# Down projection of a gated MLP by one level of Strassen's scheme, in three sweeps over PSUM

## The chip, the cores and the metric

One NeuronCore of a Trainium2 chip runs the whole program. The metric is device time in microseconds (us) of one execution; a lower number is better. The engines are named as the profile names them: PE (TensorE), DVE (VectorE), ACT (ScalarE), POOL (GpSimd) and SP (SyncE, which issues most transfers).

## The reference

One layer of a post-norm encoder, 512 tokens of 1024 channels: a token mixer (pooling, latent attention and a spatial gate), then a gated MLP. All numbers are float32. What the change touches is the end:

```python
def _conv_ffn(h, w_up, conv_w, conv_b, w_down):
    z = h @ w_up                                  # (512, 1024) @ (1024, 5632)
    ...                                           # causal depthwise convolution over three tokens
    val, gate = jnp.split(zc, 2, axis=-1)
    return (jax.nn.silu(gate) * val) @ w_down     # (512, 2816) @ (2816, 1024)

# in reference():
y = _conv_ffn(h, w_up[l], conv_w[l], conv_b[l], w_down[l])
x = _layer_norm(ALPHA * x + gt_f[:, None, :] * y) * ln_f_g[l] + ln_f_b[l]
```

gt_f is one row of 1024 numbers, the sublayer's gate, made from the condition c.

## The kernel before

Every product keeps float32 accuracy with a faster matmul type: each operand is split into a high part (a cast on ACT) and a low part (a subtraction on DVE), and mm3 issues three matmuls, high x low, low x high and high x high, onto one bank of PSUM. A matmul has 128 rows of contraction, 128 columns of the left operand and 512 of the right.

A scheduler fixes the order of the instructions on each engine when the program is built, from its own estimate of times; on the chip each engine then takes its list in that order and waits where an operand is missing.

The up projection runs over 22 chunks i of 128 hidden columns (NP = 22), value and gate half, 24 matmuls each. The epilogue of a chunk is: scale and bias on ACT out of PSUM, two DVE instructions for the other taps of the convolution (tiles zc), silu on ACT, the product of value and gate on POOL (L1203), then the split into f{i}h and f{i}l, which lie transposed: hidden columns on partitions, 512 tokens in the free dimension.

The down projection is the call of project_out at the end. It holds all eight banks of PSUM (tiles pyd: four token tiles by two halves of the 1024 output columns). For each chunk k it loads 128 rows of w_down (512 KB, by SP, into a buffer raw of which there are three), multiplies them by gt_f on POOL in two halves of 512 columns (scaled_chunk, L936), splits them (L940 on ACT, L941 on DVE), and issues 24 matmuls. The last four chunks are kept resident, so that the token tiles come to their end one after the other, and finish(t) of a tile (residual, LayerNorm, gain and bias, store) runs beside the matmuls of the next; only the last one has nothing beside it.

The row of gt_f is made beside the up projection (ada_piece, ada_rows). Tiles of the tags pt (8 buffers of 512 columns), h (16), act (48), and whi and wlo (two of 1024 columns each) are handed round.

## Time and profile before

| what | us |
|---|---|
| three runs | 1021.66, 1024.28, 1024.99; median 1024.28 |
| profiled execution, first to last instruction (span) | 1018.8 |
| median less span | 5.5 |
| PE busy in the span | 973.7 (96%) |
| DVE, ACT, POOL busy | 611.4, 384.2, 325.7 |
| first matmul of the down projection starts | 888.71 |
| its last matmul ends | 1010.34 |

The page lists no time of the profiled execution beside its span. Times in the text are us from the start of the span. A row of the time line has start, duration, engine, line, operation, output and inputs, and in brackets how long the engine sat idle before it and what ended that. A row of a group has the count, then busy time and mean ns. Line numbers are those of the kernel before.

### The profile page before, as it was taken

To read this page: it belongs to the slowest core of one execution; us is meant where nothing else is said; L and a number is where in the kernel's file an instruction comes from. 1 tells how busy PE (TensorE), PEld (TensorE's weight loads), DVE (VectorE), ACT (ScalarE), POOL (GpSimd) and SP (SyncE) were. 2 spreads that over 40 slices of the span, in tenths; PEclk is the share of its full clock that TensorE was granted. 3 is DMA by queue.
4 is the path that set the end of the run, shared out by engine and by line. 5 is a ranking of instruction groups with operands and counts; after the bars stand their busy time and mean duration, and the time that the engine had idled before them with its cause. 6 is when DMAs were issued, how large, how long until landed. Compare 5 with 4: busy or idle time off the path is not lost.

```text
span 1018.8 us, 12189 instructions
## 1 busy us (share of the span) xinstructions
PE 973.7 (96%) x4496; PEld 797.4 (78%) x4496; DVE 611.4 (60%) x931; ACT 384.2 (38%) x650; POOL 325.7 (32%) x340
## 2 busy tenths in 40 slices
PE   4789999999999999999999999899999999999996
PEld 3677778777888877788888877898888888888885
DVE  7957555548446377763343578676666665633267
ACT  3365454542224322332322233664443443412221
POOL 5564111121242054120001575512111121466664
PEclk9999999999999999999999999999999999999998
DMA  9612111118324226652223255113433343342322
GB/s 336 259 40 91 47 50 50 57 42 279 114 83 124 89 80 211 202 184 87 79 83 104 83 169 203 42 62 113 136 124 112 116 145 85 99 137 94 103 83 83
DMA packets 45276, 119.20 MB, mean 117 GB/s; under 512 B 5280, under 2 KB 8736, under 8 KB 45216
## 3 DMA queue, kind: packets, MB, share of 16 engines
q1 hardware_dynamic: 45072, 118.30, 35.8%
q8 instruction: 35, 0.57, 0.2%
q14 instruction: 25, 0.20, 0.1%
q10 hardware_dynamic: 144, 0.12, 0.0%
HBM read 116.30 MB, written 2.10 MB: 116 GB/s over the span
## 4 chain that ended last, share of the span: by engine, by line
PE 73%; DVE 9%; POOL 6%; DMA 6%; issue 4%; ACT 2%; SPq 0%; DVEq 0%; POOLq 0%; ACTq 0%
PE pzu L97 7%; PE pzu L99 7%; PE pzu L98 7%; PE pg L98 4%; PE pyd L97 4%; PE pg L99 4%; PE pg L97 4%; PE pyd L99 4%; PE pyd L98 4%; PE pu L97 3%; PE pu L99 3%; PE pu L98 3%; PE py L98 2%; PE py L99 2%; PE py L97 2%
## 5 line engine op out<-in xcount | busy, mean ns | idle before, releaser
L1203 POOL TENSOR_TENSOR zc<-zc 128x512 f32<-128x512 f32 x22 | 32.8, 1489 | 178.9 <-ACT zc L1202 178.9
L936 POOL TENSOR_TENSOR d<-d,gtfb 128x512 f32<-128x512 f32 x44 | 72.8, 1677 | 41.9 <-DMA d<-in_wdn 39.5
L298 POOL TENSOR_TENSOR mg<-mg,th 128x512 f32<-128x512 f32 x16 | 25.0, 1562 | 139.7 <-DVE th L295 120.2
L1188 DVE SCALAR_TENSOR_TENSOR zc<-pzu,cols,zc 128x511 f32<-128x511 f32 x44 | 32.8, 747 | 52.4 <-ACT zc L1185 52.4
L1185 ACT ACTIVATE zc<-pzu,cols 128x512 f32<-128x512 f32 x44 | 34.2, 779 | 72.2 <-PE pzu L99 72.2
L941 DVE TENSOR_TENSOR dl<-d,dh 128x1024 fp32r<-128x1024 f32 x18 | 29.9, 1660 | 52.3 <-ACT dh L940 52.3
L679 DVE SCALAR_TENSOR_TENSOR ada<-adar,cact,ada 128x512 f32<-128x512 f32 x56 | 52.9, 970 | 13.2 <-DMA adar<-in_ada 13.2
L90 ACT CAST wbh<-wb 128x1024 fp32r<-128x1024 f32 x24 | 25.2, 1050 | 65.7 <-PE py L99 57.2
L91 DVE TENSOR_TENSOR wgl<-wg,wgh 128x1024 fp32r<-128x1024 f32 x22 | 27.3, 1243 | 35.3 <-ACT wgh L90 34.1
L91 DVE TENSOR_TENSOR wupl<-wup,wuph 128x1024 fp32r<-128x1024 f32 x38 | 46.6, 1227 | 0.0
L91 DVE TENSOR_TENSOR wbl<-wb,wbh 128x1024 fp32r<-128x1024 f32 x24 | 35.1, 1461 | 16.3 <-ACT wbh L90 16.1
L91 DVE TENSOR_TENSOR wsgl<-wsg,wsgh 128x1024 fp32r<-128x1024 f32 x16 | 19.6, 1223 | 39.4 <-ACT wsgh L90 39.4
L940 ACT CAST dh<-d 128x1024 fp32r<-128x1024 f32 x18 | 18.9, 1051 | 60.7 <-PE pyd L99 60.6
L90 ACT CAST wuph<-wup 128x1024 fp32r<-128x1024 f32 x38 | 39.5, 1039 | 0.0
L278 ACT ACTIVATE th<-pg 128x512 f32<-128x512 f32 x22 | 13.1, 597 | 61.8 <-PE pg L99 61.8
L113 POOL TENSOR_SCALAR pw<-mv 128x1 f32<-128x1 f32 x20 | 8.2, 408 | 82.5 <-DVE mv L122 69.6
L90 ACT CAST wsgh<-wsg 128x1024 fp32r<-128x1024 f32 x16 | 16.8, 1049 | 47.0 <-PE pu L99 44.9
L1192 DVE SCALAR_TENSOR_TENSOR zc<-pzu,cols,zc 128x510 f32<-128x510 f32 x44 | 32.7, 747 | 1.3
L936 POOL TENSOR_TENSOR o<-o,gttb 128x512 f32<-128x512 f32 x16 | 27.0, 1712 | 17.5 <-DVE th L295 9.8
L734 POOL TENSOR_TENSOR asum<-apad 128x527 f32<-128x527 f32 x8 | 9.1, 1141 | 59.2 <-ACT apad L729 25.9
L600 POOL TENSOR_SCALAR pe<-pe,mx 128x128 f32<-128x128 f32 (+3 forms) x32 | 17.4, 553 | 33.4 <-DVE mx L599 33.2
L201 DVE SCALAR_TENSOR_TENSOR acc<-ada,cact,acc 128x256 f32<-128x256 f32 x48 | 27.8, 638 | 0.0
(1369 smaller groups left out, 3230.0 us busy)
## 6 DMA issues: line engine op xcount, KB each, us to landing
wup<-in_wup SPq DMA_DIRECT2D x44, 512.0 KB, 3.5
adar<-in_ada SPq DMA_DIRECT2D x64, 256.0 KB, 3.8
wb<-in_wb SPq DMA_DIRECT2D x24, 512.0 KB, 3.5
wg<-in_wg SPq DMA_DIRECT2D x22, 512.0 KB, 3.5
d<-in_wdn SPq DMA_DIRECT2D x22, 512.0 KB, 3.5
ada<-in_ada SPq DMA_DIRECT2D x32, 256.0 KB, 4.8
wsg<-in_wsg SPq DMA_DIRECT2D x16, 512.0 KB, 3.5
wa<-in_wa SPq DMA_DIRECT2D x8, 512.0 KB, 3.5
```

What stands on the lines that cost most here:

```text
L90: nc.scalar.copy(out=hi[:, :n], in_=raw[:, :n])
L91: nc.vector.tensor_tensor(out=lo[:, :n], in0=raw[:, :n], in1=f(hi[:, :n]), op=ALU.subtract)
L97: nc.tensor.matmul(o, wh, xl, start=start, stop=False)
L98: nc.tensor.matmul(o, wl, xh, start=False, stop=False)
L99: nc.tensor.matmul(o, wh, xh, start=False, stop=stop)
L679: nc.vector.scalar_tensor_tensor(out=acc[n], in0=src, scalar=cact[:, k : k + 1], in1=acc[n], op0=ALU.mult, op1=ALU.add,)
L936: nc.gpsimd.tensor_tensor(out=raw[:, c], in0=raw[:, c], in1=gt[n], op=ALU.mult)
L941: nc.vector.tensor_tensor(out=lo, in0=raw, in1=f(hi), op=ALU.subtract)
L1185: nc.scalar.activation(t, pz, AF.Identity, bias=cols[:, cc + 3 : cc + 4], scale=cols[:, cc + 2 : cc + 3])
L1188: nc.vector.scalar_tensor_tensor(out=t[:, 1:512], in0=pz[:, 0:511], scalar=cols[:, cc + 1 : cc + 2], in1=t[:, 1:512], op0=ALU.mult, op1=AL ...
L1192: nc.vector.scalar_tensor_tensor(out=t[:, 2:512], in0=pz[:, 0:510], scalar=cols[:, cc : cc + 1], in1=t[:, 2:512], op0=ALU.mult, op1=ALU.add,)
L1203: nc.gpsimd.tensor_tensor(out=val, in0=val, in1=gate, op=ALU.mult)
```

## The change

The down projection takes chunks in pairs q (NQ = 11): chunk 2q and chunk 2q + 1. With the tokens halved (rows 0 to 255 and 256 to 511) and the output columns halved, each pair is a 2 x 2 block product: A11, A21 are the halves of f{2q}, A12, A22 those of f{2q+1}; B11, B12 are the column halves of chunk 2q of w_down, B21, B22 those of chunk 2q + 1. Seven block products take the place of eight, and a block product is six matmuls (two token tiles by three):

| sweep | bank | left | right |
|---|---|---|---|
| 1 | P1 | A11 | B11 |
| 1 | P5 | A21 - A22 | B11 + B12 |
| 1 | P6 | A21 - A22 - A11 | B11 + B12 + B22 |
| 1 | P4 | A22 | B11 + B12 + B21 + B22 |
| 2 | onto P1 | A12 | B21 |
| 2 | onto P5 | A12 - A22 - (A11 - A21) | B22 |
| 3 | onto P6 | A11 - A21 | B12 + B22 |

Each row is summed over the 11 pairs. Between sweep 1 and the next, P1 is copied to SBUF (m1, ACT) and three sums with it are kept: v = P5 - P1, u = P6 + P1, w = P4 + P1 (DVE, out of PSUM). The four output blocks are sums of P1, P5, P6 with u, v, w. gt_f multiplies u, v, w (fold, on POOL) and the banks at the end (finish, on DVE) and no longer the weights.

Sums on the left are made by pair_up (POOL, three of 256 columns a pair) beside the up projection, and in second_operands. Sums of the weights are made on POOL in sweep 1, three of 512 columns a pair. B12 + B22 is made by third_sum: SP loads B12 into a raw buffer and POOL issues a second transfer that adds B22 to it while it lands. The weights are loaded once in sweep 1, the odd chunks again in sweep 2, and the right halves again for sweep 3. finish gets two more DVE instructions a tile, and for the tiles 0 to 2 the form with scale and bias on ACT and gain and bias on POOL and DVE.

The diff, cut to its core:

```diff
+    def pair_up(q):
+        fe, fo = f_t[2 * q], f_t[2 * q + 1]
+        s12 = pad_t("s12")
+        nc.gpsimd.tensor_tensor(out=s12[:, :256], in0=fe[:, 256:], in1=fo[:, 256:], op=ALU.subtract)
+        nc.gpsimd.tensor_tensor(out=s12[:, 256:512], in0=s12[:, :256], in1=fe[:, :256], op=ALU.subtract)
+        nc.gpsimd.tensor_tensor(out=fe[:, 256:], in0=fe[:, :256], in1=fe[:, 256:], op=ALU.subtract)
...
+    def third_sum(q):
+        x = wp.tile([P, D], F32, name="wdn3", tag="raw", bufs=3)
+        nc.sync.dma_start(out=x[:, :512], in_=wdn(2 * q, 1))
+        nc.gpsimd.dma_start(out=x[:, :512], in_=wdn(2 * q + 1, 1), accum_op=ALU.add)
+        t3[q] = halves_split([x[:, :512]], act_t, f"t3{q}")
+    for q in range(NQ):
+        fe, fo = f_t[2 * q], f_t[2 * q + 1]
+        r0 = load(A["wdn"][2 * q * P : (2 * q + 1) * P, :], D, "wdn")
+        r1 = [pt_t(f"wdn{n}") for n in range(2)]
+        for n in range(2):
+            nc.sync.dma_start(out=r1[n], in_=wdn(2 * q + 1, n))
+        nc.gpsimd.tensor_tensor(out=r0[:, 512:], in0=r0[:, :512], in1=r0[:, 512:], op=ALU.add)
+        nc.gpsimd.tensor_tensor(out=r1[1], in0=r1[1], in1=r0[:, 512:], op=ALU.add)
+        nc.gpsimd.tensor_tensor(out=r1[0], in0=r1[0], in1=r1[1], op=ALU.add)
...
+        product(P1, (ah[:, :256], al[:, :256]), (h0[:, :512], l0[:, :512]), first, final)
+        product(P5, (sh[:, :256], sl[:, :256]), (h0[:, 512:], l0[:, 512:]), first, final)
+        product(P6, (sh[:, 256:], sl[:, 256:]), (h1[1], l1[1]), first, final)
+        product(P4, (ah[:, 256:], al[:, 256:]), (h1[0], l1[0]), first, final)
+        if q:
+            third_sum(q - 1)
...
+    for q in range(NQ - RES):
+        ops = second_operands(q)
+        for i in range(2):
+            second(q, i, ops)
+        if q == 0:
+            fold("u", 1, 0, ALU.subtract)
...
     def finish(t, banks):
...
         for n in range(2):
+            nc.vector.tensor_tensor(out=dst[n], in0=banks[n], in1=gt_f[n], op=ALU.mult)
+            if t < 2 and n == 0:
+                nc.vector.scalar_tensor_tensor(
+                    out=dst[n], in0=x1[t][n], scalar=ALPHA, in1=dst[n], op0=ALU.mult, op1=ALU.add
+                )
+            else:
+                nc.vector.tensor_tensor(
+                    out=dst[n], in0=x1[t][n], in1=dst[n],
+                    op=ALU.subtract if t >= 2 and n == 1 else ALU.add,
+                )
             nc.vector.bn_stats(out=st[:, n, :], in_=dst[n])
...
-    project_out(
-        lambda k: A["wdn"][k * P : (k + 1) * P, :], NP, 4, a_hi, a_lo, gt_f, h_t, finish, "d"
-    )
+    for q in range(NQ - RES, NQ):
+        stay[q] = second_operands(q)
+    for i in range(2):
+        for q in range(NQ - RES, NQ):
+            second(q, i, stay[q])
+        finish(i, (P1[i], P5[i]))
+    for i in range(2):
+        c = slice(i * P, (i + 1) * P)
+        l = slice(256 + i * P, 256 + (i + 1) * P)
+        for q in range(NQ):
+            (th,), (tl,) = t3[q]
+            mm3(P6[i], s3[q][:, c], s3[q][:, l], th, tl, False, q == NQ - 1, True)
+        finish(2 + i, (P6[i], P6[i]))
```

The order of the built program holds 528 pyd matmuls before and 462 now. Three places of it matter to the prediction.

First, POOL at the seam of up and down projection. Before, zc is the product of value and gate of a chunk (the third row is that of the last chunk), and d a piece of weights times the gate:

```order
L936 TENSOR_TENSOR d<-d,gtfb_7157 128x512
L936 TENSOR_TENSOR d<-d,gtfb_7159 128x512
L1203 TENSOR_TENSOR zc<-zc 128x512
L936 TENSOR_TENSOR d<-d,gtfb_7157 128x512
L936 TENSOR_TENSOR d<-d,gtfb_7159 128x512
```

Now f_7502 and f_7575 are those products of the last two chunks, s_7577 the tile s12 of the last pair, wdn the weight sums of pairs 0 to 2:

```order
L1223 TENSOR_TENSOR f_7502<-zc 128x512
L1250 DMA wdn_7693<-in_wdn 128x512
L1261 TENSOR_TENSOR wdn_7596<-wdn_7596,wdn 128x512
L1223 TENSOR_TENSOR f_7575<-zc 128x512
L1262 TENSOR_TENSOR wdn_7595<-wdn_7595,wdn_7596 128x512
L1261 TENSOR_TENSOR wdn_7645<-wdn_7645,wdn 128x512
L1177 TENSOR_TENSOR s_7577<-f_7502,f_7575 128x256
L1260 TENSOR_TENSOR wdn<-wdn 128x512
L1262 TENSOR_TENSOR wdn_7644<-wdn_7644,wdn_7645 128x512
L1178 TENSOR_TENSOR s_7577<-s_7577,f_7502 128x256
```

The sums of pairs 0 to 2 stand between the last chunk's product and the last pair's s12. ACT at the same place, now:

```order
L1281 CAST a1h<-f_6054 128x256
L1182 CAST s10h<-s_7577 128x512
L1281 CAST a1h<-f_6133 128x256
L1281 CAST a0h<-f_5920 128x256
L1281 CAST a0h<-f_5987 128x256
```

The left operand of the first pair, a0h, stands behind the cast of the last pair's s12; PE's first row of the stage is `L97 MATMUL pyd<-wdnl,a0h 128x512`.

Second, POOL in the middle of sweep 1, now (two pairs; the L1250 rows are the adding transfers of third_sum):

```order
L1260 TENSOR_TENSOR wdn<-wdn 128x512
L1261 TENSOR_TENSOR wdn_7935<-wdn_7935,wdn 128x512
L1250 DMA wdn_7983<-in_wdn 128x512
L1262 TENSOR_TENSOR wdn_7934<-wdn_7934,wdn_7935 128x512
L1260 TENSOR_TENSOR wdn<-wdn 128x512
L1261 TENSOR_TENSOR wdn_7993<-wdn_7993,wdn 128x512
L1250 DMA wdn_8041<-in_wdn 128x512
L1262 TENSOR_TENSOR wdn_7992<-wdn_7992,wdn_7993 128x512
```

Where POOL had two products a chunk (the rows L936 above, four a pair), it has three sums and a transfer a pair, the transfer ahead of the last sum.

Third, the end of DVE's list. Before, these are the rows behind the one that reads the last matmul's bank (out_8360 is the second half of token tile 3), with that row first:

```order
L1219 SCALAR_TENSOR_TENSOR out_8360<-x_31_5451,pyd 128x512
L1222 BN_STATS st<-out_8360 128x6
L1224 BN_AGGR mv<-st 128x2
L1228 SCALAR_TENSOR_TENSOR out_8360<-out_8360,mv,lnfg_7565 128x512
L1228 SCALAR_TENSOR_TENSOR out_8359<-out_8359,mv,lnfg_7563 128x512
L1240 SCALAR_TENSOR_TENSOR out_8360<-out_8360,rs,lnfb_7569 128x512
L1240 SCALAR_TENSOR_TENSOR out_8359<-out_8359,rs,lnfb_7567 128x256
```

Now the last matmul's bank is read by the second row here (out_8632, token tile 1); out_8688 and out_8689 are token tile 2, and 28 rows follow the second, of which these are the first:

```order
L1365 TENSOR_TENSOR out_8631<-pyd,gtfb_7173 128x512
L1365 TENSOR_TENSOR out_8632<-pyd,gtfb_7175 128x512
L1365 TENSOR_TENSOR out_8688<-pyd,gtfb_7173 128x512
L1367 SCALAR_TENSOR_TENSOR out_8631<-x_10_5340,out_8631 128x512
L1365 TENSOR_TENSOR out_8689<-pyd,gtfb_7175 128x512
L1371 TENSOR_TENSOR out_8632<-x_11_5341,out_8632 128x512
L1371 TENSOR_TENSOR out_8688<-x_20_5404,out_8688 128x512
L1375 BN_STATS st<-out_8631 128x6
```

On PE the last matmul onto P6 (token tiles 2 and 3) stands 60 matmuls ahead of the last of all, which goes onto P5 of token tile 1.

145 lines of the change are left out of this document (124 added, 21 removed).

## Prediction

> **What bounds the kernel now.** I read the page first (busy shares, slices, chain), then the time line of the down projection by engine, then the groups by shape.
>
> ```profile
> span 1018.8 us, 12189 instructions
> PE 973.7 (96%) x4496; PEld 797.4 (78%) x4496; DVE 611.4 (60%) x931; ACT 384.2 (38%) x650; POOL 325.7 (32%) x340
> PEclk9999999999999999999999999999999999999998
> PE 73%; DVE 9%; POOL 6%; DMA 6%; issue 4%; ACT 2%; SPq 0%; DVEq 0%; POOLq 0%; ACTq 0%
> ```
>
> PE is busy for 96% of the span, the granted clock is full until the last slice, and PE carries 73% of the chain that ended last. In the stage that is changed PE has no gap. Two rows of the time line, the first matmul of the 24 of one chunk and of the next, and the busy times of ten microseconds of this stage (span stretch, then PE, PEld, DVE, ACT, POOL busy with their counts, clock, DMA share, GB/s):
>
> ```profile
> 966.23 0.40 PE L97 MATMUL pyd<-dl,f14h 128*128 128x512 f32 x1
> 971.72 0.39 PE L97 MATMUL pyd<-dl,f15h 128*128 128x512 f32 x1
> ```
> ```profile
> 920.00:930.00 10.00, 10.00 (x45) 8.24 (x44) 2.42 (x2) 2.10 (x2) 6.55 (x6) 1.00 0.34 107
> ```
>
> 5.49 us for 24 matmuls is 0.2288 us each. Beside it POOL is busy 6.55 of 10 us and DVE only 2.42, so matmuls are the price of this stage and POOL is the engine with the least room.
>
> **Matmuls: a gain of 15.1 us.** 528 become 462; 66 x 0.2288 = 15.1 us, all on the path as long as PE stays the bound. No other term below is a gain, except 0.8 us of idle PE that before has in the stage (888.71 to 1010.34 is 121.6 us, 528 x 0.2288 is 120.8).
>
> **The start: a loss of 13.3 us.** Where the stage begins today:
>
> ```profile
> 888.71 0.50 PE L97 MATMUL pyd<-dl,f0h 128*128 128x512 f32 x1 [0.45 <-DVE dl L941]
> ```
> ```profile
> 890.73 0.64 ACT L1202 ACTIVATE zc<-zc 128x512 f32<-128x512 f32 x1 [0.72 <-DVE zc L1192]
> 892.30 2.54 POOL L936 TENSOR_TENSOR d<-d,gtfb 128x512 f32<-128x512 f32 x2 [4.74 <-DMA d<-in_wdn]
> 894.80 1.29 POOL L1203 TENSOR_TENSOR zc<-zc 128x512 f32<-128x512 f32 x1
> ```
>
> The first down matmul runs at 888.71, right behind the up projection, since f0 was split long ago. The gating product of the last chunk, f21 (POOL, L1203), has its input at 891.37 (890.73 + 0.64) but starts at 894.80, because POOL takes its instructions in their order and two weight pieces stand ahead of it. Nothing waits for f21 then. In the changed order something does: PE's first down matmul reads a0h, ACT casts a0h after s10h, s10h needs s12 of the last pair, and that needs f21. So the first matmul waits for the end of the up projection's epilogue and for POOL's rows up to L1178. Prices alone, by shape:
>
> ```profile
> L936 POOL TENSOR_TENSOR d<-d,gtfb x44: 1283/1302/2334, 874.6 to 986.6; 128x512 f32<-128x512 f32 x44
> L941 DVE TENSOR_TENSOR dl<-d,dh x18: 1218/1578/2325, 886.5 to 978.5; 128x1024 fp32r<-128x1024 f32 x18
> L947 ACT CAST d18h<-d x2: 622/622/622, 975.5 to 976.7; 128x512 fp32r<-128x512 f32 x2
> L948 DVE TENSOR_TENSOR d20l<-d,d20h x2: 1565/1568/1571, 984.0 to 985.7; 128x512 fp32r<-128x512 f32 x2
> L83 SPq DMA_DIRECT2D d<-in_wdn x22: 327/328/328, 870.0 to 980.4; - x22
> DMA to landing us min/median/max: 3.2/3.5/4.6
> ```
> ```profile
> L1238 POOL TENSOR_TENSOR out<-out,lnfb 128x256 f32<-128x256 f32 x1 | 0.7, 747 | 0.6 <-ACT out L1237 0.6
> L125 POOL TENSOR_SCALAR rs<-mv,rs 128x1 f32<-128x1 f32 x16 | 6.0, 376 | 1.2
> ```
> ```profile
> L948 DVE TENSOR_TENSOR o4l<-o,o4h 128x512 fp32r<-128x512 f32 x2 | 1.3, 680 | 0.0
> L104 DVE TENSOR_TENSOR PTl<-ptp,PTh 128x256 fp32r<-128x256 f32 x8 | 3.2, 404 | 0.0
> L1228 DVE SCALAR_TENSOR_TENSOR out<-out,mv,lnfg 128x512 f32<-128x512 f32 x8 | 5.7, 749 | 0.1
> L1222 DVE BATCH_NORM_STATS2 st<-out 128x6 f32<-128x512 f32 x8 | 5.5, 691 | 0.2
> ```
> ```profile
> L508 ACT CAST qst<-qro 128x256 fp32r<-128x256 f32 x8 | 2.9, 405 | 3.8 <-POOL qro L501 3.8
> L1237 ACT ACTIVATE out<-out,rs 128x512 f32<-128x512 f32 x3 | 2.2, 725 | 17.9 <-POOL rs L116 17.9
> ```
>
> (The rows of tile d give least, median and most in ns; the others the mean.) POOL: 1.30 for 512 columns, 0.75 for 256. DVE: 1.22 for 1024, 0.69 for 512, 0.40 for 256, all undisturbed. ACT: 0.62 and 0.41. From 891.4 POOL has five of 512 columns and two of 256, 8.0 us, to 899.4; ACT's s10h, a1h and a0h take 1.44 to 900.8. DVE disturbs POOL twice in that time (next part), and four handovers between engines come on top: I take 902. The bounds are 900.8 and 904. 902 - 888.7 = 13.3.
>
> **What DVE and POOL cost each other.** The price of an operation is not its price alone here. The median of d20l is 1.57 us where o4l, the same shape, took 0.68. The place:
>
> ```profile
> 981.82 6.56 POOL L936 TENSOR_TENSOR d<-d,gtfb 128x512 f32<-128x512 f32 x4 [0.26 <-DMA d<-in_wdn]
> ```
> ```profile
> 983.96 3.28 DVE L948 TENSOR_TENSOR d20l<-d,d20h 128x512 fp32r<-128x512 f32 x2
> ```
>
> Four POOL operations took 6.56 us back to back (1.64 each) with one DVE operation beside each. Alone the pair would be 1.30 + 0.69 = 1.99 one after the other; so two busy engines pass through in 1.64 / 1.99 = 0.82 of their summed time, nearly as if they took turns. [...]
>
> **Sweep 1: a loss of 7.4 us.** From 891.4 on it still needs on POOL: f21, nine sums of r0, ten and eleven of the two halves of r1 (31 x 1.30) and three of 256 columns (2.3): 42.6. DVE: ten low parts of 1024 (12.2), 34 of 512 (22 of r1, 11 of the third sums, s10l: 23.5) and 22 of 256 (8.8): 44.5. Together 87.1, x 0.82 = 71.4: to 962.8. PE, begun at 902, needs 264 x 0.2288 = 60.4: to 962.4. So both are full, and anything that leaves one of them without work adds. That is the third sum: its plain load waits for a raw buffer, POOL's accumulating transfer waits for the load and holds POOL's queue (the r1 sum of the next pair stands behind it), then ACT, then DVE, ahead of the next l0. One round for two pairs: chunk load 3.5 and 0.33 to issue, two POOL sums of 1.64 (disturbed), the accumulating transfer, cast 0.62, subtraction 1.57. The accumulating transfer has no row. Nearest, 256 KB and the slowest single load (KB, us to landing):
>
> ```profile
> adar<-in_ada SPq DMA_DIRECT2D x64, 256.0 KB, 3.8
> wqr<-in_wqr SPq DMA_DIRECT2D x1, 512.0 KB, 6.9
> ```
>
> I take 3.8, the same size, and 6.9 as the far end; 0 would be the near end. With 3.8 the round is 13.1 us, 6.55 a pair, against 5.49 on PE: 1.06 x 7 pairs, once the first four are through, is 7.4. End of sweep 1 at 969.8, 7.4 later than PE alone; bounds 0 and, at 6.9 (3.1 more a round, 1.55 more a pair), 18.3. The Trainium skill (DMA: Bandwidth & Descriptors, Latency and other measured facts) puts the first byte of a transfer that GpSimd generates at about 1 us against 0.6; by it the round would be 0.4 longer and the sum 1.4 us higher; no row here shows it.
>
> **Sweeps 2 and 3: a loss of 6 us.** 198 matmuls, 45.3 us, are mixed by the order (P6's fill the waits of P1 and P5). Operands: POOL 22 sums of 256 and six gate products, 16.5 + 7.8 = 24.3; DVE 33 of 256 (13.2), eight of 1024 (9.8), six of 512 (4.1), six folds of 0.75 and six subtractions from PSUM of 0.69 (8.6): 35.7. 60.0 x 0.82 = 49.2, begun some 3 us before sweep 1 ends: to 1016. About 24 matmuls (5.5 us) come behind the last operand: last matmul at 1021, some 6 later than PE alone (1015.1). Bounds 0 and 17 (factor 1.0). ACT has a cast of 1.05 and five of 0.41 a pair, 3.1 us in the 4.1 that PE takes, and a chunk of 512 KB lands in 3.5: nothing for either.
>
> **The end: a loss of 19.5 us.** Now:
>
> ```profile
> 1009.94 0.40 PE L99 MATMUL pyd<-d21h,f21h 128*128 128x512 f32 x1
> 1010.38 0.69 DVE L1219 SCALAR_TENSOR_TENSOR out<-x,pyd 128x512 f32<-128x512 f32 x1 [0.53 <-PE pyd L99]
> 1011.10 0.69 DVE L1222 BATCH_NORM_STATS2 st<-out 128x6 f32<-128x512 f32 x1
> 1011.83 0.21 DVE L1224 BATCH_NORM_AGGREGATE mv<-st 128x2 f32<-128x12 f32 x1
> 1012.07 1.42 DVE L1228 SCALAR_TENSOR_TENSOR out<-out,mv,lnfg 128x512 f32<-128x512 f32 x2
> 1012.13 0.75 POOL L113 TENSOR_SCALAR pw<-mv 128x1 f32<-128x1 f32 x1 [1.60 <-DVE mv L1224]
> 1012.96 0.94 POOL L116 TENSOR_TENSOR rs<-pw,neghalf 128x1 f32<-128x1 f32 x1
> 1013.93 1.61 DVE L1240 SCALAR_TENSOR_TENSOR out<-out,rs,lnfb 128x512 f32<-128x512 f32 x2 [0.44 <-POOL rs L116]
> 1014.51 0.75 POOL L1238 TENSOR_TENSOR out<-out,lnfb 128x256 f32<-128x256 f32 x1 [0.62 <-ACT out L1237]
> ```
>
> The last matmul ends at 1010.34, seven DVE rows follow, and the span closes 3.3 us after the last of them, 8.5 in all. In the changed order the tiles of tokens 256 to 511 are ready 60 matmuls early, but their rows stand on DVE behind the gate product of token tile 1 that reads the last matmul's bank. So 31 DVE instructions follow it or run at its end: 22 of about 0.72 with the gap (15.8), four of 0.75 (3.0), the three aggregations and a half row (1.1), the first one 0.7: 20.6 us; five or six of them meet POOL's gain and bias products, and POOL's own chain (two pairs of row statistics at 0.75 + 0.94 + 0.38, three full products, then the last tile's 0.75 + 1.30 + 0.94 + 0.75, with ACT at 0.73 between) ends near 25. With 3.3 behind it: 28, against 8.5. Bounds 23 and 31.
>
> **Edits that cost nothing.** The gate on the weights goes (44 POOL products of 1.30 to 1.64), but POOL's new sums are in the ledgers above. pair_up on POOL (three of 256 columns a pair) lies beside 96 up matmuls, some 22 us, in which POOL has two products else; without that cover it would be 2.3 us a pair.
>
> **Sum.** -15.1 - 0.8 + 13.3 + 7.4 + 6 + 19.5 = +30.3: span 1018.8 -> 1049. The page gives no time of its execution beside the span; the median of the runs is 1024.28, 5.5 above it (launch and end, carried over): 1024.3 + 30.3 = 1054.6, said as 1055.
>
> **Rivals.** (a) The sweeps run at PE's pace, since DVE and POOL overlap better than in the one place I could read: last matmul at 902 + 105.7 = 1007.7, 1041 in all. For it: the ledgers come out level with PE at 0.82. Against: the round of the third sum. (b) Full turns, factor 1.0: sweep 1's operands to 891.4 + 87.1 = 978.5, those of sweep 2 to 1038.5, the last matmul 5 later, time about 1077. [...] (c) The accumulating transfer at 6.9: 10.9 us more: 1066. (d) Faster: PE stays the bound throughout; the waits in the ledgers, at the start and at the end are hidden and 15.1 comes through: 1009. It decides once all waits together stay under 15.1 us; the order gives 32.8 at the two ends alone, so both readings would have to be wrong. (e) The matmuls aren't fewer: excluded by the order's count of 462.
>
> **Chances.** Mine, 1046 to 1062: 0.47. (a) 0.22; (b) 0.09; (c) 0.12; (d) 0.06; partly (d), no change within 0.3% (3 us, about what a measurement here tells apart): 0.04. Slower 0.90, same 0.04, faster 0.06. The range 1036 to 1075 takes in (a), mine and (c) and leaves out (b), (d) and no change.
>
> **What would show it.** The first pyd matmul near 902, behind ACT's a0h, with POOL busy before it; in sweep 1 a pair every 6.6 us, PE waiting for DVE's low parts, and DVE's 512 columns at 1.0 to 1.6; sweep 1 over at 970; last matmul at 1021; then 28 us with PE idle and DVE full. I am wrong if PE has no gap at 889, or the span closes within 12 us of the last matmul.

## The result, and the profile after

The changed kernel takes 1075.1 us (median of four runs, 1073.8 to 1076.5) against 1023.0 for the kernel before on the same chip: a ratio of 1.051, 95% interval 1.049 to 1.053. Slower was forecast, at 1055 with a range of 1036 to 1075; the time is 20 us above the forecast and just outside the range. Three lines of the page after:

```profile
span 1073.4 us, 12434 instructions
...
PE 977.5 (91%) x4430; PEld 792.4 (74%) x4430; DVE 684.2 (64%) x1024; ACT 416.2 (39%) x731; POOL 373.1 (35%) x407
...
PEclk9899999999999999999999989999999997999895
```

The span is 1073.4, 54.6 longer than before. PE went from 96% busy to 91%. Its granted clock (a digit for each 26.8 us, in tenths) shows 7 and 8 in two slices of the down projection, 886 to 912 and 993 to 1020, where before had 9, and 5 in the last one, where PE is idle. Next, the three stretches that the prediction prices, as windows of the profile after: first sweep (first product to last), second and third sweep (to the last matmul), and close. The columns are stretch and length, then busy time and count of PE, PEld, DVE, ACT and POOL, granted clock, DMA share and GB/s:

```profile
902.20:990.10 87.90, 72.05 (x264) 53.27 (x264) 62.57 (x65) 36.81 (x69) 46.61 (x40) 0.91 0.60 159
990.10:1046.20 56.10, 50.15 (x199) 38.88 (x198) 46.56 (x66) 19.39 (x40) 28.32 (x26) 0.94 0.34 104
1046.20:1073.40 27.20, 0.00 (x0) 0.00 (x0) 22.26 (x30) 4.96 (x7) 14.67 (x17) 0.58 0.21 77
```

The loss of each is what it took beyond its matmuls at 0.2288 us each; the end is compared with the 8.5 us of before.

| loss against PE alone, us | predicted | measured | from |
|---|---|---|---|
| start | 13.3 | 13.5 | first product at 902.2 |
| first sweep | 7.4 | 27.5 | 87.9 less 264 x 0.2288 |
| sweeps two and three | 6 | 10.8 | 56.1 less 198 x 0.2288 |
| end | 19.5 | 18.7 | 27.2 less 8.5 |
| fewer matmuls, idle time before | -15.9 | -15.9 | |
| sum on the span | +30.3 | +54.6 | |

In the first sweep neither DVE (62.6 of 87.9 us) nor POOL (46.6) is full, and still PE waits. From the list of waits (who waits for whom: us in all, times, longest), and the idle time ahead of PE's rows on the time line:

```profile
PE pyd L97 <- ACT a0h L1281: 13.5, 1, 13.5
...
POOL wdn L1260 <- DMA wdn<-in_wdn: 21.9, 6, 8.6
...
POOL wdn L1250 <- DMA wdn<-in_wdn: 11.3, 3, 5.3
...
ACT t33h L1235 <- DMA wdn<-in_wdn: 9.3, 1, 9.3
```
```profile
902.24 1.22 PE L97 MATMUL pyd<-wdnl,a0h 128*128 128x512 f32 x2 [13.52 <-ACT a0h L1281]
...
916.96 0.50 PE L97 MATMUL pyd<-wdnl,a1h 128*128 128x512 f32 x1 [1.23 <-DVE wdnl L1266]
...
925.92 0.50 PE L97 MATMUL pyd<-wdl,s3h 128*128 128x512 f32 x1 [3.15 <-DVE wdl L1236]
...
944.00 0.50 PE L97 MATMUL pyd<-wdnl,s5h 128*128 128x512 f32 x1 [2.82 <-DVE wdnl L1266]
```

PE waits for DVE's low parts (wdnl, wdl), as foretold; but behind that stand POOL, which waits for transfers, and ACT, which waits for the third sum's. The wait of 3.15 us at 925.92, followed back, in order of time:

```profile
914.73 0.69 DVE L1236 TENSOR_TENSOR t31l<-wdn,t31h 128x512 fp32r<-128x512 f32 x1 [6.13 <-ACT t31h L1235]
915.45 0.33 SPq L83 DMA_DIRECT2D wdn<-in_wdn  x1
919.32 1.28 POOL L1260 TENSOR_TENSOR wdn<-wdn 128x512 f32<-128x512 f32 x1 [8.60 <-DMA wdn<-in_wdn]
922.66 4.91 DVE L1236 TENSOR_TENSOR wdl<-wdn,wdh 128x512 fp32r<-128x512 f32 x2 [4.62 <-ACT wdh L1235]
```

The low part of a third sum, late because ACT waited for its transfer, gives a raw buffer free at 915.42. SP issues the next row load at once (the trace names t31l as what released it), and POOL has stood 8.60 us for that row. Then POOL's sums come in a burst, and beside them two low parts take 4.91 us, where two alone take 1.28. PE goes on behind the first of them. The wait of 2.82 us at 944.00 stands behind one slow transfer: the adding transfer issued at 932.37 landed 7.4 us later (least, median and most of the eleven: 3.7, 4.3 and 7.4), and t33h, for which ACT stood 9.3 us, is its cast.

The last matmul and the last DVE rows:

```profile
1045.76 0.40 PE L99 MATMUL pyd<-wr10h,c10h 128*128 128x512 f32 x1
```
```profile
1067.92 1.61 DVE L1402 SCALAR_TENSOR_TENSOR out<-out,rs,lnfb 128x512 f32<-128x512 f32 x2
```

### The profile page after: what moved, and what is told of

Same layout as the page of the kernel before. It is cut to its first block, busy times and chain, and to the rows that moved or that the text cites. A ratio compares the mean times of both kernels' runs of the same rounds, so it can differ in the third digit from the quotient of the medians.

```text
span 1073.4 us, 12434 instructions
## 1 busy us (share of the span) xinstructions
PE 977.5 (91%) x4430; PEld 792.4 (74%) x4430; DVE 684.2 (64%) x1024; ACT 416.2 (39%) x731; POOL 373.1 (35%) x407
## 5 line engine op out<-in xcount | busy, mean ns | idle before, releaser
L1223 POOL TENSOR_TENSOR f<-zc 128x512 f32<-128x512 f32 x22 | 33.4, 1519 | 158.5 <-ACT zc L1221 158.5
L679 DVE SCALAR_TENSOR_TENSOR ada<-adar,cact,ada 128x512 f32<-128x512 f32 x56 | 55.7, 1021 | 13.2 <-DMA adar<-in_ada 13.1
L90 ACT CAST wbh<-wb 128x1024 fp32r<-128x1024 f32 x24 | 25.2, 1050 | 65.7 <-PE py L99 57.2
L91 DVE TENSOR_TENSOR wgl<-wg,wgh 128x1024 fp32r<-128x1024 f32 x22 | 27.3, 1243 | 35.3 <-ACT wgh L90 34.2
L91 DVE TENSOR_TENSOR wbl<-wb,wbh 128x1024 fp32r<-128x1024 f32 x24 | 35.2, 1465 | 16.3 <-ACT wbh L90 16.1
L278 ACT ACTIVATE th<-pg 128x512 f32<-128x512 f32 x22 | 13.1, 597 | 61.8 <-PE pg L99 61.8
L936 POOL TENSOR_TENSOR o<-o,gttb 128x512 f32<-128x512 f32 x16 | 26.9, 1702 | 18.2 <-DMA o<-in_wo 14.0
L1236 DVE TENSOR_TENSOR wdl<-wdn,wdh 128x512 fp32r<-128x512 f32 x20 | 24.7, 1255 | 8.2 <-ACT wdh L1235 7.6
L90 ACT CAST wgh<-wg 128x1024 fp32r<-128x1024 f32 x22 | 23.2, 1052 | 11.6 <-PE pu L99 5.7
L201 DVE SCALAR_TENSOR_TENSOR acc<-ada,cact,acc 128x256 f32<-128x256 f32 x48 | 26.8, 616 | 0.0
L1260 POOL TENSOR_TENSOR wdn<-wdn 128x512 f32<-128x512 f32 x11 | 15.9, 1447 | 29.0 <-DMA wdn<-in_wdn 21.9
```

The costliest lines, as they stand in the source:

```text
L90: nc.scalar.copy(out=hi[:, :n], in_=raw[:, :n])
L91: nc.vector.tensor_tensor(out=lo[:, :n], in0=raw[:, :n], in1=f(hi[:, :n]), op=ALU.subtract)
L201: nc.vector.scalar_tensor_tensor(out=acc[i], in0=src, scalar=cact[:, k : k + 1], in1=acc[i], op0=ALU.mult, op1=ALU.add,)
L679: nc.vector.scalar_tensor_tensor(out=acc[n], in0=src, scalar=cact[:, k : k + 1], in1=acc[n], op0=ALU.mult, op1=ALU.add,)
L936: nc.gpsimd.tensor_tensor(out=raw[:, c], in0=raw[:, c], in1=gt[n], op=ALU.mult)
L1223: nc.gpsimd.tensor_tensor(out=fi, in0=val, in1=gate, op=ALU.mult)
```

## The experiments

Each layer experiment was timed beside the kernel before. "First" is the length of the first sweep, "2+3" from its end to the last matmul, "close" from there to the span's end, all from the one profiled execution of that run. For e3 and e6 that execution took 1068.5 and 1070.3 us, 3.6 and 4.7 above the median. e8 and e12 edit nothing in the first sweep, and it takes 84.9 and 83.9 us there, after a start 4.0 and 2.9 later; so a difference of 3 to 4 us in one stage is not read as an effect of an edit.

| run | time | ratio to before (95%) | first product | first | 2+3 | close |
|---|---|---|---|---|---|---|
| changed kernel | 1075.1 | 1.051 (1.049-1.053) | 902.2 | 87.9 | 56.1 | 27.2 |
| e1 | 1069.4 | 1.045 (1.042-1.048) | 905.9 | 81.3 | 52.6 | 27.7 |
| e2 | 1064.2 | 1.040 (1.038-1.043) | 902.5 | 76.7 | 54.4 | 27.7 |
| e3 | 1064.9 | 1.042 (1.039-1.045) | 902.4 | 76.3 | 60.3 | 27.8 |
| e4 | 1076.8 | 1.053 (1.050-1.056) | 908.8 | 84.7 | 57.3 | 26.9 |
| e5 | 1048.6 | 1.025 (1.024-1.027) | 900.0 | 62.8 | 56.6 | 28.0 |
| e6 | 1065.6 | 1.043 (1.041-1.046) | 905.0 | 78.8 | 56.9 | 27.8 |
| e7 | 1069.6 | 1.046 (1.044-1.048) | 892.5 | 92.2 | 57.4 | 27.3 |
| e8 | 1070.1 | 1.047 (1.045-1.048) | 906.2 | 84.9 | 57.5 | 19.7 |
| e9 | 1023.3 | 1.001 (0.999-1.002) | | | | |
| e10 | 1039.1 | 1.016 (1.014-1.018) | 893.1 | 70.5 | 54.3 | 20.2 |
| e11 | 1038.8 | 1.016 (1.014-1.019) | 890.6 | 76.4 | 46.5 | 23.5 |
| e12 | 1071.5 | 1.048 (1.046-1.050) | 905.1 | 83.9 | 52.2 | 28.8 |
| e13 | 1034.4 | 1.012 (1.010-1.014) | 890.0 | 70.8 | 46.5 | 23.5 |
| e14 | 1032.3 | 1.009 (1.006-1.013) | 890.7 | 71.2 | 46.4 | 21.8 |

### What paces the first sweep: e1 to e6

**e1**, another place for the third sum's tile:

```diff
-        x = wp.tile([P, D], F32, name="wdn3", tag="raw", bufs=3)
+        x = pad_t("wdn3")
```

> The tile into which third_sum loads and accumulates takes a buffer of the pad kind (five, idle in the first sweep) in the place of one of the three raw buffers that the row loads use; nothing else is edited. Theory A (the first sweep of the products, 88 us in the changed kernel against 60.4 us of matmuls, is paced by the ring of three raw buffers: a row load waits until a third sum has been loaded, accumulated, copied and subtracted): the row loads come one pair earlier and the sweep takes 70 to 78 us, so 1057 to 1065 us against 1075. Rival B (the pace is VectorE and GpSimd sharing a port, the sum on which my forecast rested): the same work on both, so 1073 to 1077 us. Rival C (the accumulating transfer itself, 3.3 to 4.2 us from issue to landing, on which ScalarE waits in order): nothing of it is removed, so 1070 to 1077 us.

6.6 us of the sweep and 5.7 of the time: less gain than A gives, more than B, and just more than C. (The sweep starts 3.7 later, so its end comes only 2.9 earlier.) The time line shows what came up behind the ring. DVE and POOL of e1, around PE's longest wait in that sweep:

```profile
931.99 3.53 DVE L1236 TENSOR_TENSOR wdl<-wdn,wdh 128x512 fp32r<-128x512 f32 x1 [5.77 <-ACT wdh L1235]
935.44 3.47 DVE L1236 TENSOR_TENSOR t34l<-wdn,t34h 128x512 fp32r<-128x512 f32 x1
```
```profile
931.00 1.53 POOL L1260 TENSOR_TENSOR wdn<-wdn 128x512 f32<-128x512 f32 x1
932.22 1.52 POOL L1262 TENSOR_TENSOR wdn<-wdn,wdn 128x512 f32<-128x512 f32 x1
933.45 1.51 POOL L1261 TENSOR_TENSOR wdn<-wdn,wdn 128x512 f32<-128x512 f32 x1
```

A low part that takes 0.68 alone stands with 3.53 us while POOL runs sums at its own pace of 1.23 from start to start.

**e2**, no accumulating transfer:

```diff
-        nc.gpsimd.dma_start(out=x[:, :512], in_=wdn(2 * q + 1, 1), accum_op=ALU.add)
```

> Leaves out the accumulating transfer of third_sum (eleven of 256 KB, issued by GpSimd), so the third operand is B12 alone; loads, casts and products stay. A: a raw buffer is held some 5 us shorter for each pair, and the ring turns faster, 8 to 15 us of the sweep: 1060 to 1067 us. B: GpSimd loses 11 issues of 0.88 us that move no data through the shared port: 1072 to 1076 us. C: the sweep goes to nearly the matmuls' own pace, 62 to 68 us: 1050 to 1056 us.

A's number. C, the transfer's own time as the one cause (1050 to 1056), is out: without any adding transfer the sweep still takes 76.7. How the gain divides into the buffer held, POOL's queue and the wait for the landing, e2 does not show.

**e3**, no sums of weights on POOL:

```diff
-        nc.gpsimd.tensor_tensor(out=r0[:, 512:], in0=r0[:, :512], in1=r0[:, 512:], op=ALU.add)
-        nc.gpsimd.tensor_tensor(out=r1[1], in0=r1[1], in1=r0[:, 512:], op=ALU.add)
-        nc.gpsimd.tensor_tensor(out=r1[0], in0=r1[0], in1=r1[1], op=ALU.add)
```

> Leaves out the three sums of down weights that GpSimd makes for each pair (33 instructions of 128x512, lines 1260 to 1262), so the products run on the raw rows; all transfers stay. A: the transfers and the raw buffers set the pace, so at most 8 us of the sweep goes: 1067 to 1075 us. B: GpSimd's 33 x 1.2 us no longer share the port, VectorE runs free, and the sweep goes to the matmuls' pace, 62 to 66 us: 1049 to 1054 us. C: as A, 1068 to 1075 us.

Between A and B. **e5**, e1's and e3's edits together:

> e1 and e3 together: third_sum's tile in the pad kind, and the three GpSimd sums of weights of each pair left out (the products run on the raw rows). In e1 the first sweep took 81.3 us, in e3 76.3, against 87.9 in the changed kernel. If two limits lie one behind the other (A, the raw ring with its in-order queues; B, GpSimd keeping VectorE from the port), each hides the gain of removing the other, and both together bring the sweep to 61 to 66 us: 1048 to 1055 us. If a third thing sets the pace (the clock that falls after gaps, SP's queue, ScalarE), the sweep stays above 70 us and the time above 1058 us.

Two limits that hide each other: 6.6 us of the sweep for the one alone, 11.6 for the other, 25.1 for both (5.7, 10.2 and 26.5 us of the time), and the sweep is 2.4 us from PE alone. Those 2.4 are the clock: PE is busy for all of the 62.8 us, at a granted 0.96. The first sweep as one window in e1, e3 and e5:

```profile
905.90:987.20 81.30, 69.37 (x265) 53.95 (x266) 71.10 (x72) 39.21 (x71) 52.31 (x40) 0.89 0.60 167
```
```profile
902.40:978.70 76.30, 66.01 (x264) 51.65 (x264) 40.02 (x63) 31.87 (x60) 11.87 (x15) 0.95 0.67 180
```
```profile
900.00:962.80 62.80, 62.80 (x265) 51.44 (x266) 43.63 (x70) 38.20 (x71) 15.78 (x17) 0.96 0.79 234
```

In e1 DVE is busy for 71.1 of 81.3 us (72 instructions), in e5 for 43.6 of 62.8 (70): the 27.5 us between them are, nearly all, what DVE's instructions take longer beside POOL's sums. In e3 DVE is at 40.0 of 76.3 and POOL at 11.9: neither is full, and as e5 differs from e3 only in the third sum's tile, it is the raw ring with its transfers that costs 13.5 us there. One thing e3 and e5 leave together: without the sums, POOL's step between transfer and cast is gone as well as its load on the port. No run parts these two.

**e4** works the third operand out of sums in SBUF:

```diff
-        x = wp.tile([P, D], F32, name="wdn3", tag="raw", bufs=3)
-        nc.sync.dma_start(out=x[:, :512], in_=wdn(2 * q, 1))
-        nc.gpsimd.dma_start(out=x[:, :512], in_=wdn(2 * q + 1, 1), accum_op=ALU.add)
-        t3[q] = halves_split([x[:, :512]], act_t, f"t3{q}")
+        r0, s = raws.pop(q)
+        x = r0[:, :512]
+        nc.gpsimd.tensor_tensor(out=x, in0=s, in1=x, op=ALU.subtract)
+        t3[q] = halves_split([x], act_t, f"t3{q}")
```

> Works the third operand out from what is in SBUF: B12+B22 is the second sum (B11+B12+B22) less B11, one GpSimd subtraction of 128x512 in place of two transfers and a raw buffer for each pair; same output. A: the raw ring serves row loads alone and the sweep takes 66 to 74 us: 1053 to 1062 us. B: GpSimd gets 11 x 1.2 us more on the shared port: 1078 to 1088 us. C: as A or better, 1050 to 1058 us.

A's gain does not come, and B's range, from 1078, begins just above the 1076.8. The sweep is 3.2 us shorter after a start 6.6 later. The edit takes no raw buffer for the third sum, but it does not free the loads: the row and the sum that POOL subtracts must now stay until it has done so. SP's loads of r1 stood 24.6 us in six waits (the longest 10.9) for that subtraction, and the row loads stand behind them on SP. Eleven POOL instructions more go to the port besides. One limit was loaded in the place of another.

**e6**, the three sums on DVE (`nc.vector` for `nc.gpsimd` in e3's three lines):

> The three sums of weights of each pair go from GpSimd to VectorE; same output. B (GpSimd's instructions keep VectorE out, and a 0.68 us instruction becomes 1.8 to 3.5 us): VectorE's pair is 4.0 + 3 x 0.68 = 6.0 us undisturbed against the 7.4 of the changed kernel, the sweep 72 to 78 us (the ring is still there, e3 had 76.3): 1060 to 1067 us. The ledger of my forecast (the summed time of both engines times 0.82 is what counts, and it falls only by 3 x (1.3 - 0.68) a pair): 1064 to 1070 us. A alone: 1073 to 1077 us.

A alone is refuted (9.5 us gained with the same transfers); B's range and the ledger's both hold 1065.6, so e6 does not tell these two apart.

### What the port costs: m1, m2, m3

> Not the layer: a short program of chains, read from its trace alone. Sixteen additions of 128x512 (f32, both operands in SBUF) on VectorE alone, sixteen on GpSimd alone, then 32 on VectorE beside 16 on GpSimd; the same with GpSimd in pauses, with one VectorE operand in PSUM, with one tensor operand only, with ScalarE copies in VectorE's place; four accumulating transfers of 256 KB one after the other; eight runs of 60 matmuls with 0 to 8 VectorE additions between them. Strict turns (B): beside each other one addition of each in 0.6 + 1.25 = 1.85 us, so 16 GpSimd additions take 30 us. The factor 0.82 of my forecast: 1.52 us, 24 us. Starving (GpSimd keeps the port from one addition to the next): 20 us with two or three VectorE additions in them. An operand in PSUM or a single tensor operand, and ScalarE: no effect, 20 us and VectorE at 0.6. Accumulating transfer: 0.88 us on GpSimd's queue, 3.3 to 4.2 to landing. Matmuls: after pauses of over 2.3 us some 15 at 0.43 us in place of 0.23, after shorter ones none.

Groups of m1 by shape (count, busy time, mean ns): DVE alone, POOL alone; both at once (vb, gb); DVE with one operand in PSUM (vd) beside POOL (gd); DVE with one tensor operand (ve) beside POOL (ge):

```profile
L71 DVE TENSOR_TENSOR va<-va,x 128x512 f32<-128x512 f32 x15 | 10.4, 693 | 0.5
...
L71 POOL TENSOR_TENSOR ga<-ga,x 128x512 f32<-128x512 f32 x15 | 18.9, 1262 | 1.2
...
L71 DVE TENSOR_TENSOR vb<-vb,x 128x512 f32<-128x512 f32 x31 | 36.5, 1178 | 1.1
...
L71 POOL TENSOR_TENSOR gb<-gb,x 128x512 f32<-128x512 f32 x15 | 23.8, 1588 | 1.2
L71 DVE TENSOR_TENSOR vd<-vd,ps 128x512 f32<-128x512 f32 x31 | 21.3, 687 | 1.1
...
L71 POOL TENSOR_TENSOR gd<-gd,x 128x512 f32<-128x512 f32 x15 | 19.0, 1267 | 1.2
...
L109 DVE TENSOR_SCALAR ve<-ve 128x512 f32<-128x512 f32 x31 | 28.3, 912 | 1.1
```

What DVE and POOL take turns at when both read two operands from SBUF is called the port here. POOL's 16 additions beside DVE took 26.8 us (38.1 to 64.9), one of each in 1.67: 0.86 of the 0.69 + 1.26 = 1.95 that they take alone, near the 0.82 of the forecast and between its 24 us and the 30 of strict turns. In that time DVE's instruction takes 2.4 times its own. With an operand in PSUM nothing is lost on either side (0.69 and 1.27). The Trainium skill (SBUF — State Buffer, Who interferes with whom) says the same of an instruction with at most one SBUF input outside the modes that use two ports, and m1 agrees with 0.69 and 1.27. Two expectations of m1 missed, the single tensor operand and the limit of 2.3 us for PE's pauses; both are taken up in the last section.

> Not the layer: chains of additions without dependence on one another, read from the trace alone. In e1 a 128x512 subtraction on VectorE took 3.5 us while GpSimd ran sums back to back, and in e10 two 128x256 subtractions on GpSimd stand with 17.1 us while VectorE ran back to back. Both engines beginning together, 32 and 16 additions of 128x512; GpSimd in full run with 13, VectorE joining with 4 after the seventh; VectorE in full run with 32, GpSimd joining with 2 of 128x256 after the first. Turns as in the dependent chains of m1 (1.67 us for one addition of each): VectorE's four take some 6 us beside GpSimd's, GpSimd's two some 2 to 3 us. If the engine that issues without a pause keeps the other out: VectorE's four wait for the end of GpSimd's run (4 to 8 us for the first of them), and GpSimd's two take most of VectorE's 20 us.

> Not the layer: as m2, but with the instructions of the kernel: on VectorE low parts of splits (f32 and fp32r read, fp32r written), on GpSimd two differences of 128x256 that join after VectorE's run of 26 has begun, then a run of 13 sums in place of 128x512 that VectorE joins with 4 after the first; all of it first without and then with ScalarE's casts beside it. If it is the format or the casts that let one engine keep the other out: GpSimd's two take over 10 us in the one variant, VectorE's four 2 us and more each. If turns are kept as in m2 (GpSimd's two in 2.2 us, VectorE's four in 6.7): neither format nor casts is the reason, and the 3.5 us and 16 us of single instructions in the layer stay without a cause.

Turns in both. Four DVE additions that join POOL's run in m2; two POOL ones that join DVE's run:

```profile
L69 DVE TENSOR_TENSOR vb<-eb,x 128x512 f32<-128x512 f32 x4 | 6.7, 1740 | 8.7 <-POOL eb L85 8.7
L69 POOL TENSOR_TENSOR gc<-ec,x 128x256 f32<-128x256 f32 x2 | 2.2, 1134 | 1.5 <-DVE ec L90 1.5
```

1.74 each on DVE, 1.13 each on POOL: about one instruction of the other engine is waited for. m3 gives the same 1.74 and 1.1 to 1.2 with splits and with casts beside them. But in the layer there are rows far outside turns: the changed kernel's wdl, least, median and most in ns, and POOL's differences of the second sweep in e10:

```profile
L1236 DVE TENSOR_TENSOR wdl<-wdn,wdh x20: 675/686/3523, 896.8 to 983.3; 128x512 fp32r<-128x512 f32 x20
```
```profile
L1325 POOL TENSOR_TENSOR s<-f x11: 732/927/16388, 941.6 to 990.5; 128x256 f32<-128x256 f32 x11
```

3.5 us on DVE, and 16.4 on POOL while DVE ran without a pause for some 15 us. What lets one engine keep the other out there stays open; neither the format nor ScalarE's casts nor independence of the instructions does it by itself.

### Start, close, gate: e7, e8, e9

**e7** splits a0 three iterations before the end of the up projection:

```diff
+        if i == NP - 3:
+            a0 = left_split(0, act_t)
...
-        alloc = act_t if q == 0 else h_t
-        ah = alloc(f"a{q}h")
...
+        ah, al = a0 if q == 0 else left_split(q, h_t)
```

> The split of a0 (pair 0's left operand) is written three iterations before the end of the up projection, so that the first down matmul waits neither for the last gating product nor for s10; same output. If the operands of the sweep set its end (A and B), starting PE 12 us earlier moves little: first down matmul at 889 to 893, sweep 1 over where it was, 1070 to 1076 us. If the terms of my forecast add (13.3 us at the start by itself), 1061 to 1065 us.

The first product comes 9.7 us earlier, the sweep ends 5.4 earlier: it is 4.3 us longer. The time, 1069.6, lies just under the first range and well above the second. A gain at the start is partly eaten where operands set the pace; terms that the forecast adds are not separate.

**e8** writes the third sweep and finish(2), finish(3) ahead of the resident pairs:

```diff
-        if t < TT - 1:
+        if t != 1:
...
-    for i in range(2):
-        for q in range(NQ - RES, NQ):
-            second(q, i, stay[q])
-        finish(i, (P1[i], P5[i]))
-
     for i in range(2):
...
         finish(2 + i, (P6[i], P6[i]))
+
+    for i in range(2):
+        for q in range(NQ - RES, NQ):
+            second(q, i, stay[q])
+        finish(i, (P1[i], P5[i]))
```

> The third sweep and the closing rows of tokens 256 to 511 are written ahead of the last three pairs of the second sweep and the closing rows of tokens 0 to 255, whose second tile now takes the short closing path; same output. By my reading of the end (27.4 us after the last matmul, because rows that were ready stand behind the one that reads its bank) the close shrinks to 10 to 14 us and VectorE takes the other rows beside PE: 1058 to 1064 us. Rival: VectorE is full until the last matmul, the rows push the operands of the second sweep later, and the last matmul moves by as much: 1070 to 1076 us.

The close shrinks by 7.5, not by 13 to 17, and the last matmul comes 2.4 later, after a first product that is 4 later. The time, 1070.1, lies in the rival's range and not in that of my reading: DVE is busy 51.7 us of sweeps two and three (46.6 in the changed kernel), which take 57.5 for 56.1. Still, 5.0 us are gained. So my reading of the end was right in kind and too hopeful in size: the gain and bias products of tiles 2 and 3 still fall behind the last matmul, and DVE's there stand with 1.74 us beside POOL's.

**e9** is the kernel before with the gate on the outputs alone:

```diff
-        for n in range(2):
+        for n in range(2 if gt else 0):
...
+            nc.vector.tensor_tensor(out=dst[n], in0=py[n], in1=gt_f[n], op=ALU.mult)
...
-        lambda k: A["wdn"][k * P : (k + 1) * P, :], NP, 4, a_hi, a_lo, gt_f, h_t, finish, "d"
+        lambda k: A["wdn"][k * P : (k + 1) * P, :], NP, 4, a_hi, a_lo, None, h_t, finish, "d"
```

> The kernel before with one part of the change alone: the gate is multiplied onto the outputs in the closing rows (two VectorE products more per token tile) and GpSimd's 44 products on down weights go; no Strassen. By my steps the matmuls stay at PE's pace and only the last tile's products are on the path: 0.7 to 1.5 us more, 1022 to 1026 us. If GpSimd's products had held the stage up unseen: 1015 to 1020 us.

No difference: moving the gate costs nothing in the kernel before, so the loss comes with the Strassen part.

### Edits together: e10 to e14

**e10** joins the edits of e1, e6, e7 and e8.

> e1, e6, e7 and e8 together: the third sum's tile in the pad kind, the sums of weights on VectorE, a0 split early, the second half of the tokens closed first; same output. VectorE has 6.0 us a pair where PE has 5.49, so the first sweep takes 66 to 70 us from 890 on; the second and third as they were (56 us), the close 15 to 20: 1033 to 1044 us. If the gains hide one another as the single edits did: 1052 to 1060 us.

36 us against the changed kernel, as expected (1039.1); the single gains add to 5.7 + 9.5 + 5.5 + 5.0 = 25.7. What each edit hid from the others comes out once all are in.

**e11** adds to e10:

```diff
-        nc.vector.tensor_tensor(out=r0[:, 512:], in0=r0[:, :512], in1=r0[:, 512:], op=ALU.add)
+        nc.gpsimd.dma_start(out=r0[:, 512:], in_=wdn(2 * q, 0), accum_op=ALU.add)
...
-        nc.gpsimd.tensor_tensor(out=x[:, :256], in0=fo[:, :256], in1=fo[:, 256:], op=ALU.subtract)
-        nc.gpsimd.tensor_tensor(out=x[:, :256], in0=x[:, :256], in1=fe[:, 256:], op=ALU.subtract)
+        nc.vector.tensor_tensor(out=x[:, :256], in0=fo[:, :256], in1=fo[:, 256:], op=ALU.subtract)
+        nc.vector.tensor_tensor(out=x[:, :256], in0=x[:, :256], in1=fe[:, 256:], op=ALU.subtract)
...
-        if q == 0:
-            fold("u", 1, 0, ALU.subtract)
...
+                nc.vector.tensor_tensor(
+                    out=dst[n], in0=banks[n], in1=dst[n], op=ALU.subtract if n else ALU.add
+                )
+                nc.vector.tensor_tensor(out=dst[n], in0=dst[n], in1=gt_f[n], op=ALU.mult)
...
```

> e10 and more: B11+B12 is made by an accumulating transfer onto the loaded row (no engine's time but 0.88 us of GpSimd's queue), the differences of activations of the second sweep go from GpSimd to VectorE, and the kept terms of the first sweep are added to the banks before the gate (six GpSimd products and six VectorE rows become six VectorE rows). GpSimd then keeps VectorE out almost nowhere before the close. First sweep at PE's 5.49 a pair, 890 to 952; sweeps two and three 46 to 50 us, to 1000; the close 20 to 24 us with more rows on VectorE: 1024 to 1032 us. If transfers in the raw ring set the pace again: 1040 to 1050 us.

Sweeps two and three are at PE's pace (46.5 for 45.3), as expected; the first sweep, expected at 62, is at 76.4, and the time, 1038.8, lies between the two ranges. **e12** is the changed kernel with e11's edits to the second sweep alone, **e13** is e11 without its accumulating transfer, **e14** is e13 with `nc.vector` for `nc.gpsimd` in the gain and bias products of finish:

> The changed kernel with one part of e11 alone: the differences of activations of the second sweep on VectorE and not on GpSimd, and the kept terms of the first sweep added to the banks before the gate (no GpSimd products, no folds); same output. If GpSimd's 22 differences and six products, keeping VectorE out, make the loss in sweeps two and three (55.8 us for 45.3 us of matmuls): these sweeps take 46 to 49 us, the close gets 1 to 3 us longer by the rows added there: 1066 to 1072 us. If the loss came from operands that are late from the first sweep: 53 to 56 us and 1074 to 1079 us.

> e10 with e12's edit (e11 without the accumulating transfer for B11+B12). If e11's first sweep (76 us against 70.5 in e10) was longer because its accumulating transfers held the raw ring, the sweep is 69 to 72 us here, sweeps two and three 46 to 48, the close 21 to 24: 1030 to 1036 us. If VectorE's differences in the second sweep push the first sweep's rows back: 1037 to 1042 us.

> e13 with GpSimd's gain and bias products of the close (three tiles, six products of 128x512) on VectorE. VectorE gets 6 x 0.68 = 4.1 us more, and loses the waits for the port (0.5 to 1.1 us in six of its rows in e11, 4 us): within 1.5 us of e13. If the port is worse than that: 2 to 4 us faster.

e13's first sweep is back at 70.8, so making B11+B12 by a transfer had cost 5.6 us against DVE's sum; that the ring is where it cost them is the expectation's reading. In e12 sweeps two and three are 3.9 of their 10.8 us shorter, no more than the spread of one profile, and at 52.2 they lie between the two expectations, while the time, 1071.5, lies in the first one's range. With the edits of e10 beside it (e13) they come to 46.5. A first sweep without delay is not enough for that: in e5 it takes 62.8, and sweeps two and three still 56.6 with POOL's work in them. e14 can't be told from e13 (the intervals overlap). The windows of e14:

```profile
890.70:961.90 71.20, 65.13 (x265) 49.78 (x266) 67.03 (x110) 42.09 (x79) 14.37 (x14) 0.98 0.77 235
961.90:1008.30 46.40, 45.90 (x198) 36.65 (x196) 40.84 (x83) 18.80 (x38) 2.07 (x5) 1.00 0.36 105
1008.30:1030.10 21.80, 0.02 (x1) 0.00 (x0) 17.53 (x30) 4.45 (x7) 4.16 (x8) 0.59 0.26 97
```

It is 43 us better than the changed kernel and still 0.9% slower than the kernel before. Against before: -15.9, start +2.0, first sweep +10.8, sweeps two and three +1.1, close +13.3, together +11.3, from 1018.8 to its span of 1030.1. In the first sweep DVE has become the fullest engine, 67.0 of 71.2 us (PE 65.1). In sweeps two and three PE is the bound, 45.9 of 46.4. The close, where DVE is busy for 17.5 of 21.8 and PE idle, is now the largest loss. No version here beat the kernel before.

## Why the prediction was right or wrong

- **Direction, start, end.** The path f21, s12, s10h, a0h gave the first product at 902.2 (902 predicted); after the last matmul DVE and POOL ran for 27.2 us (28). e9 bears out for the kernel before that moving the gate costs nothing.
- **The step that failed: the first sweep's round of 13.1 us for two pairs.** The loss was sized as 1.06 us for each of 7 pairs, 7.4; it was 27.5, and the sweep was over at 990.1 and not at 970. The last product of pair 0 ends at 911.4, of pair 3 at 935.7 and of pair 10 at 990.1. So the first four pairs, which I let pass free, lost 11.5 us (33.5 for 22.0), and the other seven took 7.77 each against the 6.55 of the round and PE's 5.49: 16.0 in place of 7.4. Raw buffers and r1's tiles were late from the first pairs on: from 900 to 931 SP stood 10.5 us for DVE's wdl ahead of loads of r1, and 5.7 for t30l and t31l ahead of loads into raw buffers. And I took the ledger of the port (0.82 of the sum, "to 962.8") and the ring's round as two ceilings of which the higher counts. If that were so for the sweep as a whole, taking the lower one away would gain nothing; but e1 and e3 each gained (5.7 and 10.2 us of the time), and e5, both together, far more than their sum (26.5; of the sweep's 27.5 it gained 25.1). The rows behind 914.73 show the two as links of one chain: a late transfer leaves POOL idle, then low parts meet a burst of sums, and a low part that takes 2.36 us and not 0.68 (t33l) keeps a raw buffer that much longer from the next load. How much of the sums' part is the port, and how much POOL's step in the chain, stays open.
- **The factor 0.82 was right as a price of one pair of instructions** (m1: 0.86), and a wrong tool for a chain: it prices both engines together, but PE, ACT and the buffers wait for DVE's part alone, which in m1 became 2.4 times as long. In the changed kernel's first sweep DVE's 65 instructions took 62.6 us, where e5's 70 took 43.6. Most of its 512 columns took 0.69 and some 1.8 to 3.5, not 1.0 to 1.6 throughout. Rival (b), full turns at 1.0, came nearest in time with 1077, by luck: m1 gives 0.86, and DVE was busy 71% of the sweep, not full.
- **Rival (c), the slow accumulating transfer,** fails as a cause by itself: the median landing is 4.3 us after the issue in the changed kernel (4.0 in m1; 3.8 taken, 6.9 the rival's), and e2 leaves 16.3 of the 27.5 us. One of the eleven, at 7.4, does stand behind PE's wait at 944.00.
- **Sweeps two and three: 10.8 for 6.** The bounds of 0 and 17 hold it. e12 gives 3.9 to POOL's work, no more than one profile's spread; in e13 nearly all of it goes. Which of the edits that e13 has besides takes the rest was not separated.
- **The clock was no part of the forecast.** Before, PE had no gap here and full speed; the sum has no term for it, and no reason why it should stay full through the gaps that it forecast. After, a stretch at half speed followed each wait of 2.4 us or more: one after the start's wait and five of 3.4 us later, three of them in the first sweep (last section). While PE worked at half speed in the first sweep it lost up to some 7.5 us, an estimate: half of the 4.9 us of the first stretch that lie in the sweep and of three times 3.4. How much of that would have been waiting anyway was not separated.
- **The time beside the span.** I carried 5.5 us from a median over a span of another execution. The profiled run of the changed kernel took 1075.3 with a span of 1073.4: 1.9. On the span the error is 24.3, and this slip hid 3.6 of it.

## What to carry to other kernels

Where operands pass through a ring of buffers, a shared port and in-order queues, do not price these apart and take the highest: one that lengthens an instruction also lengthens the hold on the buffer, and removing either alone shows only a part (6.6, 11.6, both 25.1). Count the engine that prepares operands before the engine that is relieved: here 66 matmuls saved 15.1 us, and the sums and splits that they cost made DVE the fullest engine of the first sweep in the best version (e14). Rows of the close that are ready early gain less than their number while the other engine runs beside them: in e8 three of DVE's took 1.74 us each behind the last matmul.
